# Strassen's seven products in a down-projection: another order, sums made where a block is split, products gathered in SBUF

## The chip, the cores and the metric

One NeuronCore of one Trainium2 chip runs the whole program. The metric is the device time of one execution in microseconds (us), the median of 3 runs. Below, PE is the matrix engine, ACT the scalar engine, DVE the vector engine, SP the queue that issues most of the transfers.

## The reference

Two residual layers on 256 tokens of width 2048, all in float32. Layer 0 mixes tokens with stick-breaking attention, layer 1 with an indexer that selects keys. After each mixer stands the same MLP, and the change touches only the second product of that MLP:

```python
for i in range(DEPTH):                      # DEPTH = 2
    h = rms_norm(x, norm_mix[i])
    x = x + mixer_i(h)                      # stick-breaking, then DSA
    h = rms_norm(x, norm_mlp[i])
    x = x + jnp.square(jax.nn.relu(h @ w_up[i])) @ w_down[i]
```

`w_up` is 2048 x 8192 and `w_down` 8192 x 2048.

## The kernel before

**The work list.** The program is one long list of items. An item is one block of weights, 256 rows by 512 columns, with the matmuls that use it. Activations are held transposed and split in two float32r parts, high and low; a weight block is split the same way. Each product of two 128-row tiles is three matmuls: high x high, high x low, low x high. An ordinary item therefore has 12 matmuls (2 token tiles x 2 row tiles x 3).

**What is done for an item** (the loop at the end of `trunk`, and `load` and `split`, L963 to L996). At item i the program emits, in this order: the split of item i+2, the load of item i+7, the extra loads that hang on the item (`early`), the item's matmuls, the steps that hang on it (`post`), and delayed steps that are due (`later`). A split is a copy on ACT to the high part (L89) and a subtraction on DVE for the low part (L993), with `after` behind it. The two parts lie in a buffer `w` of which there are three: the copy for item i+2 waits until PE has finished item i-1. Loaded blocks lie in `wraw`, of which there are five.

**The order on each engine.** The program is not run in the order in which it is written: a list scheduler puts each engine's instructions in an order before the run, by when it reckons each to be ready, and the earlier one in the program goes first among those that are ready. An instruction wrapped in `keep` cannot stand ahead of the instruction emitted just before it on its engine. Instructions without `keep` (both halves of a split among them) may go earlier or later. On the chip each engine then takes its instructions strictly in that fixed order.

**The MLP.** The 8192 hidden columns are handled in four quarters f. `up(f)` makes 2048 hidden columns in 32 items. A finished group of 512 columns goes through `up_done`: two transposes on DVE (L169), a write to DRAM and a read back, then squared ReLU on DVE (L343), a high part on ACT (L348) and a low part on DVE (L353), each a fixed number of items later. `down(f)` multiplies the quarter by its 2048 rows of `w_down`. The order is up 0, up 1, down 0, up 2, down 1, up 3, down 2, down 3. So the last two groups of the `up` ahead of a `down` still have their ReLU and low parts inside the first pair of that `down`.

**A pair.** `down_pair(f, n)` handles two column groups of 512, G and H, for both token tiles. Of eight row blocks six are ordinary items (G0 to G5, H0 to H5). The other two row blocks (0 and 2) are taken together as a 2 x 2 by 2 x 2 block product in Winograd's form of Strassen's scheme: seven products s1 to s7 of 6 matmuls each in place of eight. The list `TURNS` says how the 19 items follow each other. There are 15 pairs: 8 in the first MLP and 7 in the second, whose last two column groups are done in the ordinary way.

The sums of activations that the scheme needs are made once for each quarter (`sums`). The sums of weight blocks are made in each pair on DVE: three in the `form` of s5, s6 and s7 (L489), one behind the split of s6 (L494). The four blocks are loaded by extra loads on SP (L385) into four tiles of their own, and the seven s-items take nothing from `wraw`.

The products s2, s3 and s4 add to one accumulator each, in PSUM, together with G and H. The products s1, s5, s6 and s7 are shared by several outputs, so each goes to one of two PSUM buffers `aux`, and from there to the residual stream `xs`: s1 is copied to a tile `u` (ACT) and added to one block of `xs`, s5 is added to two, s7 to two at once, and s6 is added to `u`, which is then added to three (L466, L482). That is seven DVE instructions in a pair. When G5 or H5 is done, `down_done` adds its accumulator to `xs` (L305).

## Time and profile before

| | |
|---|---|
| median of 3 runs | 2077.98 us (2077.17 to 2078.2) |
| profiled execution | 2077.52 us, its span 2075.8 us |
| granted PE clock | full |
| transfers | 464.83 MB, mean 224 GB/s |

Times in the profile are us from the start of the span. PE stands for matmuls, PEld for the weight loads that go ahead of them and overlap them. A timeline row holds a start, a duration, the engine, the line, what is written and read, how many instructions are merged in the row, and in brackets how long the engine sat idle before it and what ended that. A matmul's shown duration includes its way through the array, so matmuls overlap in the rows; what counts is the distance from one start to the next.

### The profile page before, as it was taken

How to read it: one execution, taken by the hardware profiler on the slowest of the kernel's cores; microseconds unless marked ns; L12 is line 12 of the kernel's file. 1: busy time of each engine (PE TensorE's matmuls, PEld its weight loads, DVE VectorE, ACT ScalarE, POOL GpSimd, SP SyncE). 2: the span in 40 equal slices, each digit the busy share in tenths (PEclk: the TensorE clock that was granted, in tenths of full speed). 3: DMA queues.
4: the chain of work that ended last, by engine and by line, in shares of the span. 5: the costliest groups of instructions: out<-in, count | busy, mean ns of one | idle time of the engine just before them, and what ended most of it. 6: DMA issues, size and time to landing. Idle time of an engine off the chain costs nothing.

```text
span 2075.8 us, 24805 instructions
## 1 busy us (share of the span) xinstructions
PE 2062.2 (99%) x9164; PEld 1696.1 (82%) x9164; DVE 1467.0 (71%) x1611; ACT 1026.2 (49%) x1233; POOL 26.3 (1%) x71
## 2 busy tenths in 40 slices
PE   9999999999999999999999999999999999999999
PEld 7888888888888888888887788878888888888887
DVE  5556555666696687688885898666669668867885
ACT  6555554544444454445554566554445444444453
POOL 0100000000000000000000000000000000000000
PEclk9999999999999999999999999999999999999999
DMA  9787856988766966876679688498876687677655
GB/s 305 229 235 213 236 172 199 298 250 245 219 208 216 256 206 209 233 211 209 200 216 264 184 250 258 143 265 271 246 242 205 212 238 221 209 216 224 204 176 165
DMA packets 477466, 464.83 MB, mean 224 GB/s; under 512 B 269665, under 2 KB 279969, under 8 KB 477345
## 3 DMA queue, kind: packets, MB, share of 16 engines
q1 hardware_dynamic: 469488, 455.81, 72.3%
q10 hardware_dynamic: 7856, 7.45, 1.2%
q8 instruction: 71, 1.16, 0.2%
q14 instruction: 51, 0.41, 0.1%
HBM read 425.90 MB, written 37.22 MB: 223 GB/s over the span
## 4 chain that ended last, share of the span: by engine, by line
PE 88%; DVE 6%; DMA 2%; issue 2%; ACT 1%; SPq 1%; DVEq 0%; ACTq 0%
PE acc L290 20%; PE acc L291 20%; PE acc L289 20%; PE acc L427 19%; DVE w L993 3%; PE aux L446 2%; DVE xs L466 2%; PE acc L446 1%; ACT w L89 1%; SPq L175 1%; DMA td<-jx 1%; PE acc L259 1%; PE aux L858 1%; DMA wraw<-in_w_up_dram 1%; DVE u L482 0%
## 5 line engine op out<-in xcount | busy, mean ns | idle before, releaser
L993 DVE TENSOR_TENSOR w<-wraw,w 128x1024 fp32r<-128x1024 f32 (+1 forms) x680 | 826.8, 1217 | 506.8 <-ACT w L89 502.0
L89 ACT ACTIVATE w<-wraw 128x1024 fp32r<-128x1024 f32 (+1 forms) x680 | 720.5, 1060 | 860.4 <-PE acc L291 565.0
L290 PE MATMUL acc<-w,xT 128*128 128x512 f32 x1632 | 638.1, 391 | 1.7 <-DVE w L993 1.5
L289 PE MATMUL acc<-w,xT 128*128 128x512 f32 x1632 | 637.1, 391 | 1.9 <-ACT xT L200 1.0
L291 PE MATMUL acc<-w,xT 128*128 128x512 f32 x1632 | 636.3, 390 | 0.0
L427 PE MATMUL acc<-w,hT 128*128 128x512 f32 x2160 | 512.3, 390 | 4.4 <-DVE w L993 3.4
L427 PEld LDWEIGHTS acc<-w,hT 128*128 128x128 f32 x2160 | 404.0, 188 | 96.1 <-DVE w L993 12.4
L289 PEld LDWEIGHTS acc<-w,xT 128*128 128x128 f32 x1632 | 306.4, 188 | 66.8 <-ACT w L89 2.1
L290 PEld LDWEIGHTS acc<-w,xT 128*128 128x128 f32 x1632 | 306.4, 188 | 66.5 <-DVE w L993 2.7
L291 PEld LDWEIGHTS acc<-w,xT 128*128 128x128 f32 x1632 | 306.4, 188 | 64.1 <-issue 0.7
L89 ACT ACTIVATE w<-b 128x1024 fp32r<-128x1024 f32 x105 | 111.5, 1062 | 83.9 <-PE acc L427 61.1
L993 DVE TENSOR_TENSOR w<-b,w 128x1024 fp32r<-128x1024 f32 x105 | 127.8, 1217 | 26.8 <-ACT w L89 26.8
L289 PE MATMUL acc<-w,oT 128*128 128x512 f32 x256 | 100.3, 394 | 0.0
L290 PE MATMUL acc<-w,oT 128*128 128x512 f32 x256 | 99.5, 390 | 0.0
L291 PE MATMUL acc<-w,oT 128*128 128x512 f32 x256 | 99.0, 391 | 0.0
L446 PE MATMUL aux<-w,S 128*128 128x512 f32 x270 | 68.5, 389 | 0.0
L446 PEld LDWEIGHTS aux<-w,S 128*128 128x128 f32 x270 | 50.7, 188 | 10.5
L289 PEld LDWEIGHTS acc<-w,oT 128*128 128x128 f32 x256 | 48.1, 188 | 10.2 <-ACT junk L796 0.4
L290 PEld LDWEIGHTS acc<-w,oT 128*128 128x128 f32 x256 | 48.1, 188 | 9.8
L291 PEld LDWEIGHTS acc<-w,oT 128*128 128x128 f32 x256 | 48.1, 188 | 9.8
L489 DVE TENSOR_TENSOR b<-b,b 128x1024 f32<-128x1024 f32 x45 | 54.8, 1217 | 0.2
L169 DVE STREAM_TRANSPOSE jx<-acc 128x512 f32<-128x512 f32 x68 | 44.6, 694 | 12.0 <-PE acc L291 9.2
(176 smaller groups left out, 1200.0 us busy)
## 6 DMA issues: line engine op xcount, KB each, us to landing
wraw<-in_w_up_dram SPq DMA_DIRECT2D x256, 512.0 KB, 4.4
wraw<-in_w_down_dram SPq DMA_DIRECT2D x196, 512.0 KB, 4.7
wraw<-in_w_in_a_dram SPq DMA_DIRECT2D x94, 512.0 KB, 4.6
wraw<-in_w_in_b_dram SPq DMA_DIRECT2D x64, 512.0 KB, 4.6
td<-jx SPq DMA_DIRECT2D x240, 128.0 KB, 4.3
b<-in_w_down_dram SPq DMA_DIRECT2D x60, 512.0 KB, 4.9
jx<-td SPq DMA_DIRECT2D x45, 512.0 KB, 6.1
wraw<-in_w_out_a_dram SPq DMA_DIRECT2D x32, 512.0 KB, 3.7
```

Of the source, the lines that this page charges most:

```text
L89: pin(act.activation(o, i, AF.Copy, scale=scale))
L169: dve.transpose(y[:, m:m + k, :].rearrange("p k f -> p (k f)"), part)
L175: keep(nc.sync.dma_start(d[:, :, :, a, :].rearrange("b j n i -> j n b i"), y[32 * a:32 * a + 32].rearrange("p n (b i) -> p n b i", b=4)))
L259: pin(pe.matmul(accs[key][t], L[:, j, part, t * P:(t + 1) * P], wx[:, j, :], start=(j == 0 and n == 0), stop=False))
L289: pin(pe.matmul(acc[t], L[:, k, 0, ts], wh[:, j, :], start=(k == 0), stop=False))
L290: pin(pe.matmul(acc[t], L[:, k, 0, ts], wl[:, j, :], start=False, stop=False))
L291: pin(pe.matmul(acc[t], L[:, k, 1, ts], wh[:, j, :], start=False, stop=(k == (end if t else KT) - 1)))
L427: keep(pe.matmul(acc[t], L[:, k, part, ts], wx[:, j, :], start=(i, j, m) == (0, 0, 0), stop=(i, j, m) == (len(qs) - 1, KB - 1, 2)))
L446: keep(pe.matmul(p, left(part, j), wx[:, j, :], start=to is None and (j, m) == (0, 0), stop=to is None and (j, m) == (KB - 1, 2)))
L466: dve.scalar_tensor_tensor(xc, p, sec["rs2"][:, t:t + 1], xc, op0=OP.mult, op1=OP.add)
L489: dve.tensor_sub(x, block(a), block(b))
L993: pin(dve.tensor_sub(wl[:, a], raw[:, a], wh[:, a].bitcast(F32)))
```

## The change

The seven products come in another order, s1 and s3 early and s6 and s5 side by side:

```
before  G0 s1 G1 H0 s5 G2 H1 s7 G3 H2 G4 s6 H3 s3 s2 H4 s4 G5 H5
after   G0 H0 s1 G1 s3 H1 G2 s6 s5 H2 s7 G3 H3 s2 G4 H4 s4 G5 H5
```

Three of the four blocks of weights (of s1, s2, s3) are now loaded into `wraw` like any item's. Only the fourth keeps a tile of its own, Y, loaded by one extra load. The four sums of weight blocks are made behind the split of the item whose block they need, with `keep`: one behind s1, two behind s3, one behind s2, into tiles X, Z and Y. The shared products gather in a tile E of four blocks in SBUF, one block for each token tile and column group: s1 is copied there, s6, s5 and s7 are added with one instruction each, and E is added to `xs` with two instructions, behind G3 and H3. All of these have `keep`. That is five DVE instructions for the products in place of seven.

```diff
-TURNS = "G0 s1 G1 H0 s5 G2 H1 s7 G3 H2 G4 s6 H3 s3 s2 H4 s4 G5 H5".split()
+TURNS = "G0 H0 s1 G1 s3 H1 G2 s6 s5 H2 s7 G3 H3 s2 G4 H4 s4 G5 H5".split()
...
+            def load_y():
+                keep(nc.sync.dma_start(new("Y"), block(1, qa)))
+
+            def t1(b11):
+                keep(dve.tensor_sub(new("X"), sec["Y"], b11))
+
+            def t2_t3(b22):
+                keep(dve.tensor_sub(new("Z"), b22, sec["X"]))
+                keep(dve.tensor_sub(sec["Y"], b22, sec["Y"]))
+
+            def t4(b21):
+                keep(dve.tensor_sub(sec["Z"], b21, sec["Z"]))
 
             def p1(p):
-                sec["u"] = sec["pool"].tile([P, 512], F32, name="u", bufs=1)
-                copy(sec["u"], p)
-                into(0, (0,), p)
+                sec["E"] = sec["pool"].tile([P, 4, 512], F32, name="E", bufs=1)
+                keep(act.activation(sec["E"][:, 0], p, AF.Copy))
+
+            def p6(p):
+                keep(dve.tensor_add(sec["E"][:, 1], p, sec["E"][:, 0]))
 
             def p5(p):
-                for t in range(2):
-                    into(t, (1,), p)
+                keep(dve.tensor_add(sec["E"][:, 2], p, sec["E"][:, 1]))
 
             def p7(p):
-                into(1, (0, 1), p)
...
+                E = sec["E"].rearrange("p (a b) e -> p a b e", a=2)
+                keep(dve.tensor_add(E[:, :, 1], p.unsqueeze(1).to_broadcast([P, 2, 512]),
+                                    sec["E"][:, 1:3]))
+
+            def into(t):
+                xc = xs[:, t, 1024 * n:1024 * n + 1024].rearrange("p (c e) -> p c e", c=2)
+                E = sec["E"].rearrange("p (c t) e -> p c t e", t=2)[:, :, t]
+                keep(dve.scalar_tensor_tensor(xc, E, sec["rs2"][:, t:t + 1], xc,
+                                              op0=OP.mult, op1=OP.add))
...
+            seven["s1"].after, seven["s3"].after, seven["s2"].after = t1, t2_t3, t4
             for name in TURNS:
...
-            for name, col, q, at in (("b11", 0, qa, 8), ("b22", 1, qb, 6), ("b21", 0, qb, 5), ("b12", 1, qa, 3)):
-                items[base - at].early.append(lambda name=name, col=col, q=q: load_block(name, f, n, col, q))
+            items[base - 8].early.append(load_y)
+            for t in range(2):
+                items[base + TURNS.index(("G3", "H3")[t])].post.append(lambda t=t: into(t))
...
             if it.after is not None:
-                it.after()
+                it.after(raw)
```

## The prediction

> **What bounds the kernel now.** I read the page's engine shares first, then the list of waits, then two pairs as windows, then the order of time inside the first pair.

> ```profile
> span 2075.8 us, 24805 instructions
> PE 2062.2 (99%) x9164; PEld 1696.1 (82%) x9164; DVE 1467.0 (71%) x1611; ACT 1026.2 (49%) x1233; POOL 26.3 (1%) x71
> L489 DVE TENSOR_TENSOR b<-b,b 128x1024 f32<-128x1024 f32 x45 | 54.8, 1217 | 0.2
> ...
> PEld acc L427 <- DVE w L993: 12.4, 19, 1.2
> ```
> ```profile
> 559.60:602.30 42.70, 42.53 (x188) 34.83 (x187) 39.18 (x38) 22.61 (x22) 0.00 (x0) 1.00 0.69 216
> 602.30:644.90 42.60, 42.49 (x188) 34.87 (x187) 35.37 (x35) 20.73 (x20) 0.00 (x0) 1.00 0.61 200
> ```

> PE works through the whole span, and the change leaves its matmuls alone: 19 items and 186 matmuls in a pair before and after. So the time can move only by PE's waits. In the pairs these are the 12.4 us in which a weight load waited for the low half of a split; L489 runs 45 times, three in a pair, so there are 15 pairs. The two windows are the two pairs of one quarter (length, then busy time of PE, PEld, DVE, ACT): DVE is busy 39.2 of 42.7 us in the first, 35.4 of 42.6 in the second. DVE has little to spare there, and what stands ahead of a split in its queue decides.

> The next rows give the durations of the whole argument.

> ```profile
> 560.60 1.31 DVE L169 STREAM_TRANSPOSE jx<-acc 128x512 f32<-128x512 f32 x2
> 561.83 1.18 DVE L993 TENSOR_TENSOR w<-wraw,w 128x1024 fp32r<-128x1024 f32 x1
> 562.34 1.52 PE L446 MATMUL aux<-w,hT 128*128 128x512 f32 x6
> 562.54 1.06 ACT L89 ACTIVATE w<-wraw 128x1024 fp32r<-128x1024 f32 x1 [1.65 <-PE acc L427]
> 562.94 1.22 DVE L343 SCALAR_TENSOR_TENSOR jx<-jx 128x1024 f32<-128x1024 f32 x1
> 563.70 5.60 PE L427 MATMUL acc<-w,hT 128*128 128x512 f32 x24
> 563.96 0.60 ACT L89 ACTIVATE u<-aux 128x512 f32<-128x512 f32 x1 [0.35 <-PE aux L446]
> 564.46 1.05 ACT L89 ACTIVATE w<-b 128x1024 fp32r<-128x1024 f32 x1
> 565.41 1.05 ACT L348 ACTIVATE hT<-jx 128x1024 fp32r<-128x1024 f32 x1
> 566.34 0.74 DVE L466 SCALAR_TENSOR_TENSOR xs<-aux,rs,xs 128x512 f32<-128x512 f32 x1
> 566.67 1.06 ACT L89 ACTIVATE w<-wraw 128x1024 fp32r<-128x1024 f32 x1 [0.22 <-ACT hT L348]
> 567.00 1.21 DVE L993 TENSOR_TENSOR w<-b,w 128x1024 fp32r<-128x1024 f32 x1
> 568.13 1.22 DVE L353 TENSOR_TENSOR hT<-jx,hT 128x1024 fp32r<-128x1024 f32 x1
> 569.14 1.52 PE L446 MATMUL aux<-w,S 128*128 128x512 f32 x6
> 569.27 1.22 DVE L993 TENSOR_TENSOR w<-wraw,w 128x1024 fp32r<-128x1024 f32 x1
> ```
> ```profile
> 578.53 1.28 DVE L466 SCALAR_TENSOR_TENSOR xs<-aux,rs,xs 128x1024 f32<-128x1024 f32 x1
> 579.73 1.21 DVE L993 TENSOR_TENSOR w<-wraw,w 128x1024 fp32r<-128x1024 f32 x1
> ...
> 585.76 1.06 ACT L89 ACTIVATE w<-b 128x1024 fp32r<-128x1024 f32 x1 [1.63 <-PE acc L427]
> 586.85 1.23 DVE L993 TENSOR_TENSOR w<-b,w 128x1024 fp32r<-128x1024 f32 x1 [0.33 <-ACT w L89]
> 587.99 0.68 DVE L482 TENSOR_TENSOR u<-aux,u 128x512 f32<-128x512 f32 x1
> 588.60 1.22 DVE L993 TENSOR_TENSOR w<-b,w 128x1024 fp32r<-128x1024 f32 x1
> 589.73 1.94 DVE L466 SCALAR_TENSOR_TENSOR xs<-u,rs,xs 128x512 f32<-128x512 f32 x2
> 591.59 1.22 DVE L993 TENSOR_TENSOR w<-wraw,w 128x1024 fp32r<-128x1024 f32 x1
> ...
> 592.30 0.39 PE L427 MATMUL acc<-w,hT 128*128 128x512 f32 x1
> 592.86 2.79 PE L427 MATMUL acc<-w,hT 128*128 128x512 f32 x11 [0.17 <-DVE w L993]
> 595.49 1.52 PE L446 MATMUL acc<-w,hT 128*128 128x512 f32 x6
> ```

> **A matmul** takes 0.2267 us from start to start: 24 from 563.70 to 569.14. An ordinary item is thus 2.72 us, an s-item 1.36. **The copy** for item i+2 starts 0.20 us after the first matmul of item i (562.34, 562.54): it had waited for the buffer of item i-1. **The subtraction** starts 1.10 us after the copy (585.76, 586.85) if DVE is free. **DVE back to back** moves on every 1.13 us for 1024 columns (567.00, 568.13, 569.27), every 0.61 for the 512-column add (587.99, 588.60), every 1.20 for a 1024-column addition to `xs` (578.53, 579.73), and two transposes take 1.23. **PE goes on** 1.27 us after the subtraction started (591.59, 592.86).

> The last rows are the regular wait of a pair before: H4. Behind two adjacent s-items its second matmul was due at 592.30 + 0.23 = 592.53 and ran at 592.86, 0.33 late, because the two additions of `u` (589.73 to 591.59) stood ahead of its subtraction. The next item began at 595.49, where 592.30 + 12 x 0.2267 = 595.02 was due: 0.47 lost, so a wait costs 0.14 us more than its length. The second window is 0.1 shorter; I take 0.42 for the mean. In 15 pairs: 6.3 us. What else of the 12.4 us lies in the pairs I leave as it is.

> **The change part by part.** *Gone:* the additions of `u` in front of H4. Products cost DVE before 3 x 0.66 + 1.20 (s1, s5, s7) + 0.61 + 0.66 + 1.20 (s6) = 5.65 us in a pair, after 2 x 0.61 + 3 x 1.20 = 4.82: 0.83 less. New forms, such as a 1024-column add of a product into E, are priced by the nearest row (578.53, 1.20). If PE is waiting for nothing, this is worth nothing, so its gain is at most the 0.42 at H4. The adjacent items are now s6 and s5, and the split behind them is H2's: subtraction at 1.30 us after the start of s6, due (2.72 + 0.23 - 1.27) = 1.68 after it, with s6's addition emitted behind it. No wait there.

> *Loads:* 60 blocks as before; 45 of them now pass through the five `wraw` buffers, and load 15 hangs on its own. The shortest five items in a row, s1 G1 s3 H1 G2, last 10.9 us, and a block lands 4.7 to 4.9 us after issue:

> ```profile
> wraw<-in_w_down_dram SPq DMA_DIRECT2D x196, 512.0 KB, 4.7
> b<-in_w_down_dram SPq DMA_DIRECT2D x60, 512.0 KB, 4.9
> ```

> Loads on SP behind a late sum (the block of s3 is free only after the two sums) still have that lead. I take 0 here, and up to 0.3 us a pair for the range; a gain is excluded, since no wait above names these loads.

> *Sums with a fixed place, the part that decides.* Count from G0's first matmul: H0 2.72, s1 5.44, G1 6.80, s3 9.52, H1 10.88. The copy of s3 starts at 5.44 + 0.20 = 5.64, its subtraction at 6.74. Behind it, by `keep`, stand the two new sums at 7.87 and 9.00, and DVE is free at 10.13. H1's copy waits for s1 and stands behind the copy of product s1 (0.50, 563.96 to 564.46): 7.50, so its subtraction could go at 8.60, when the first sum is running and the second already stands ahead. It goes at 10.13; PE gets it at 11.40 and wanted it at 10.88 + 0.23 = 11.11. Wait 0.29, lost 0.43. Before, these sums floated into DVE's idle time; `keep` holds them behind s3's split although their other inputs lie ready long before. This holds for all pairs.

> In the first pair behind an `up` (three quarters in two MLPs: **six pairs**) the held-back ReLU work adds to it. Its low part (L353, 568.13) is now emitted behind the two sums, at 10.13, and H1's subtraction comes behind it. On ACT the high part stood behind the next copy (564.46, 565.41); likewise now copy of s3 5.64, high part 6.59, product copy 7.6, H1's copy 8.1, subtraction ready at 9.2. So it goes at 11.26, PE gets it at 12.53: wait 1.42, lost 1.56. That the low part goes first is what 568.13 shows: G2's copy had started at 566.67, its subtraction could have gone at 567.77, and the low part went ahead of it.

> Further on in these pairs (all starts 1.56 later: s6 17.88, s5 19.24, H2 20.60, s7 23.32, G3 24.68): H2's subtraction 19.18, addition of s6 20.31, s7's subtraction 20.92, addition of s5 22.05, ReLU of the last group 22.66, G3's subtraction 23.79. PE gets it at 25.06 and wanted it at 24.91: wait 0.15, lost 0.29. Then H3's subtraction 24.92, addition of s7 26.05, low part 27.25, s2's subtraction 28.38, the fourth sum 29.51, E to `xs` 30.64, G4's subtraction 31.84. PE gets it at 33.11 and wanted it at 29.92 + 1.85 + 0.23 = 32.00: wait 1.11, lost 1.25. Together 3.10 us. In the other nine pairs the same chain, without ReLU, brings G4's subtraction just in time (29.28 + 1.27 = 30.55 against 30.58).

> **Sum:** 6 x 3.10 + 9 x 0.43 = 22.5 us new, 6.3 us gone: +16.2. The profiled execution took 2077.52 us, 0.46 below the median of 2077.98, so I forecast 2077.5 + 16.2 = **2093.7 us**.

> The rows have DVE moving on every 1.13 us though one instruction lasts 1.22. [...]

> **The rivals.** *Overtaking (2 in 10).* H1's and G4's subtractions are not held by `keep`; the scheduler may see them ready first and put them ahead of the low part and of E's additions. Then the six pairs lose about what the nine do: 15 x 0.43 = 6.45 against 6.3, so 2077.7 us, no change. For: 588.60, where a subtraction went ahead of the additions of `u`, emitted earlier but still waiting for 587.99. Against: 568.13.

> *Gain (2 in 10).* The mechanism is H1's subtraction ahead of the second sum, whose result s7 needs only five items later. It decides at 9.84 us: a subtraction that starts earlier costs PE nothing (11.11 - 1.27). Then the 6.3 us of H4 are gone and nothing takes their place: 2071.2 us. For: DVE's load falls by 0.83 us a pair. Against: the second sum is emitted earlier and ready earlier.

> *Worse (1.5 in 10).* The high part goes ahead of s3's copy, and E's additions slide ahead of G4 in the other pairs too: about 0.5 more in each of six pairs and 0.4 in nine, 2093.7 + 6.6 = 2100.3 us.

> *Nothing happens to the time (inside the overtaking case).* If DVE's queue comes out so that each wait only moves from H4 to H1, the new order and E are real and the time is the same.

> **How the numbers follow.** Forecast 4.5 in 10, worse 1.5, overtaking 2, gain 2. So slower by over 0.2% (about what a measurement of this kernel can tell from no change, 4.2 us) 0.6, within it 0.2, faster 0.2. The forecast's own range is 2087 to 2098. The whole one reaches to the gain's 2071 below, which leaves a deeper gain out, and above to 2102, the worse case with a little of the loads.

> **What would show it.** Right: PE waits at H1's second matmul in every pair, 1.4 us in the six and 0.3 in the nine; a second wait at G4 in the six; two L489-like sums, and in the six the low part, between s3's and H1's subtractions; no wait at H4. Wrong: the low part or the second sum behind H1's subtraction, or pairs as short as 42.2 us. A wait for a `wraw` load in the pairs would mean that I priced the loads wrongly.

## The result and the profile after

The changed kernel takes **2100.9 us** (median of 4 runs, 2098.77 to 2105.26) against 2078.09 us before (4 runs): ratio 1.0112, 95% interval 1.0095 to 1.013. It is slower, by 22.8 us. The profiled execution took 2101.37 us, 23.85 more than that of before. In the page's engine shares PE has the same 9164 matmuls, and DVE got lighter by 12.3 us, 0.82 in each of 15 pairs:

```profile
span 2099.6 us, 24844 instructions
...
PE 2068.1 (99%) x9164; PEld 1697.4 (81%) x9164; DVE 1454.7 (69%) x1581; ACT 1026.3 (49%) x1233; POOL 26.0 (1%) x71
```

So the loss is waiting. The list of waits of after shows for whom: weight loads of the plain products (L419 now) waited 37.2 us for the low half of a split (L994 now), three times the 12.4 of before, in twice the number of waits. The second row is the time that PE itself stood before those matmuls, 22.7 us (3.4 before).

```profile
PEld acc L419 <- DVE w L994: 37.2, 38, 3.3
...
PE acc L419 <- DVE w L994: 22.7, 25, 2.8
```

The same two pairs as windows: the first pair grew from 42.70 to 45.52 us, the second from 42.60 to 42.90 (length, then busy time of PE, PEld, DVE, ACT).

```profile
558.78:604.30 45.52, 43.12 (x187) 34.67 (x186) 38.58 (x36) 22.50 (x22) 0.00 (x0) 1.00 0.65 206
604.30:647.20 42.90, 42.74 (x188) 34.93 (x187) 34.42 (x33) 20.73 (x20) 0.00 (x0) 1.00 0.55 183
```

If each distance from one matmul start to the next is taken, less the bare 0.2267 us, and summed over the plain products, before has 10.4 us too much and after 34.5. The difference, 24.1, is the whole loss. Where it sits is told by the first pair's timelines, DVE first, then PE, then ACT.

```profile
565.75 1.23 DVE L994 TENSOR_TENSOR w<-wraw,w 128x1024 fp32r<-128x1024 f32 x1 [0.94 <-ACT w L89]
566.89 1.22 DVE L469 TENSOR_TENSOR Z<-wraw,X 128x1024 f32<-128x1024 f32 x1
568.03 1.22 DVE L470 TENSOR_TENSOR Y<-wraw,Y 128x1024 f32<-128x1024 f32 x1
569.16 1.22 DVE L353 TENSOR_TENSOR hT<-jx,hT 128x1024 fp32r<-128x1024 f32 x1
570.30 2.36 DVE L994 TENSOR_TENSOR w<-wraw,w 128x1024 fp32r<-128x1024 f32 x2
```
```profile
569.66 0.39 PE L419 MATMUL acc<-w,hT 128*128 128x512 f32 x1
571.58 1.66 PE L419 MATMUL acc<-w,hT 128*128 128x512 f32 x6 [1.52 <-DVE w L994]
```
```profile
563.71 1.06 ACT L348 ACTIVATE hT<-jx 128x1024 fp32r<-128x1024 f32 x1 [0.94 <-DVE jx L343]
564.68 1.04 ACT L89 ACTIVATE w<-wraw 128x1024 fp32r<-128x1024 f32 x1
```

This is H1. s3's subtraction runs at 565.75; behind it stand the two sums and the ReLU's low part; H1's subtraction comes at 570.30. H1's first matmul ran on time at 569.66; the second needs the low half and was due 0.23 later, at 569.89. It ran at 571.58, 1.69 late. On ACT the ReLU's high part (563.71) stood ahead of s3's copy (564.68).

Later in the same pair, at G4, DVE and then PE:

```profile
587.38 1.22 DVE L994 TENSOR_TENSOR w<-wraw,w 128x1024 fp32r<-128x1024 f32 x1
588.51 1.23 DVE L473 TENSOR_TENSOR Z<-wraw,Z 128x1024 f32<-128x1024 f32 x1
589.65 1.29 DVE L493 SCALAR_TENSOR_TENSOR xs<-E,rs,xs 128x1024 f32<-128x1024 f32 x1
590.85 1.23 DVE L994 TENSOR_TENSOR w<-wraw,w 128x1024 fp32r<-128x1024 f32 x1
```
```profile
590.87 0.39 PE L419 MATMUL acc<-w,hT 128*128 128x512 f32 x1
592.13 2.14 PE L419 MATMUL acc<-w,hT 128*128 128x512 f32 x8 [0.87 <-DVE w L994]
```

Between s2's and G4's subtractions lie the fourth sum and the first addition of E to `xs`; G4's second matmul ran 1.03 late. The four first pairs of quarters 0 and 1 look like this one, each with 0.15 more at G3. In the second pairs, and in the first pairs of quarter 3, H1 waits 0.32 and G4 not at all, but for the places named next. No wait is left at H4, and none names a load into `wraw` for the pairs.

Three places are worse than this regular picture. In quarter 2 the first addition of the next sums of `hT` (L390), which has no `keep`, slid in ahead of s3's subtraction. DVE stood 1.13 us at it, until a write to DRAM had read its tile (`td<-jx`), and the whole queue in front of H1 began 1.3 us later than in the regular pair. DVE of after, then the PE row at H1:

```profile
916.42 1.23 DVE L390 TENSOR_TENSOR jx<-hT 128x1024 f32<-128x1024 f32 x1 [1.13 <-DMA td<-jx]
...
917.56 1.22 DVE L994 TENSOR_TENSOR w<-wraw,w 128x1024 fp32r<-128x1024 f32 x1
...
922.10 2.36 DVE L994 TENSOR_TENSOR w<-wraw,w 128x1024 fp32r<-128x1024 f32 x2
...
923.38 5.99 PE L419 MATMUL acc<-w,hT 128*128 128x512 f32 x18 [2.85 <-DVE w L994]
```

H1 waited 3.01 us there and 2.78 in MLP 1. The first of these waits had a sequel. The windows of after (length, busy times of five engines, then the granted clock and the DMA share) show the clock at half for the 3 us that follow, and back after:

```profile
924.80:927.80 3.00, 3.00 (x9) 2.33 (x8) 2.22 (x5) 0.20 (x1) 0.00 (x0) 0.50 0.82 292
927.80:929.80 2.00, 2.00 (x10) 1.67 (x9) 1.11 (x1) 0.86 (x1) 0.00 (x0) 0.99 0.15 58
```

In that stretch the matmuls started every 0.427 us, which cost about 1.5 us. The second place is quarter 2's second pairs, where the last part of the same sums (L399) stood in front of G4: 1.06 each. The third is MLP 0's last pair, where the low parts of the columns turned for the next mixer (L206, four at 1066.87 and four more at 1069.59) stood between splits, in DVE's queue: G3 ran 1.41 late, and G4 behind it 1.50.

```profile
1066.87 1.67 DVE L206 SCALAR_TENSOR_TENSOR xT<-jx,gains,xT 128x256 fp32r<-128x256 f32 x4
1068.45 1.22 DVE L994 TENSOR_TENSOR w<-wraw,w 128x1024 fp32r<-128x1024 f32 x1
1069.59 1.67 DVE L206 SCALAR_TENSOR_TENSOR xT<-jx,gains,xT 128x256 fp32r<-128x256 f32 x4
```

### The profile page after: what moved, and what is told of

The parts are those of the page before. It is cut to its first block, busy times and chain, and to the rows that moved or that the text cites. A ratio compares the mean times of both kernels' runs of the same rounds, so it can differ in the third digit from the quotient of the medians.

```text
span 2099.6 us, 24844 instructions
## 1 busy us (share of the span) xinstructions
PE 2068.1 (99%) x9164; PEld 1697.4 (81%) x9164; DVE 1454.7 (69%) x1581; ACT 1026.3 (49%) x1233; POOL 26.0 (1%) x71
## 3 DMA queue, kind: packets, MB, share of 16 engines
q8 instruction: 72, 1.18, 0.2%
## 4 chain that ended last, share of the span: by engine, by line
PE 86%; DVE 8%; issue 3%; ACT 1%; DMA 1%; SPq 0%; DVEq 0%
PE acc L289 21%; PE acc L290 21%; PE acc L291 21%; PE acc L419 16%; DVE w L994 3%; PE aux L438 1%; PE acc L438 1%; ACT w L89 1%; DVE Y L470 1%; PE acc L259 1%; DVE hT L353 1%; DVE jx L343 1%; DVE xs L493 1%; DVE Z L469 1%; PE aux L859 1%
## 5 line engine op out<-in xcount | busy, mean ns | idle before, releaser
L994 DVE TENSOR_TENSOR w<-wraw,w 128x1024 fp32r<-128x1024 f32 (+1 forms) x725 | 880.8, 1218 | 540.9 <-ACT w L89 534.1
L89 ACT ACTIVATE w<-wraw 128x1024 fp32r<-128x1024 f32 (+1 forms) x725 | 768.3, 1060 | 921.6 <-PE acc L291 587.6
L419 PE MATMUL acc<-w,hT 128*128 128x512 f32 x2160 | 518.1, 392 | 22.7 <-DVE w L994 22.7
L419 PEld LDWEIGHTS acc<-w,hT 128*128 128x128 f32 x2160 | 403.6, 188 | 120.6 <-DVE w L994 37.2
L169 DVE STREAM_TRANSPOSE jx<-acc 128x512 f32<-128x512 f32 x68 | 44.7, 696 | 14.4 <-PE acc L291 12.8
L438 PE MATMUL acc<-w,hT 128*128 128x512 f32 x180 | 45.7, 389 | 0.0
L305 DVE SCALAR_TENSOR_TENSOR xs<-acc,rs,xs 128x512 f32<-128x512 f32 x56 | 39.4, 745 | 8.6 <-PE acc L419 8.6
L438 PEld LDWEIGHTS acc<-w,hT 128*128 128x128 f32 x180 | 33.8, 188 | 7.0
## 6 DMA issues: line engine op xcount, KB each, us to landing
wraw<-in_w_up_dram SPq DMA_DIRECT2D x256, 512.0 KB, 4.2
wraw<-in_w_down_dram SPq DMA_DIRECT2D x241, 512.0 KB, 4.8
wraw<-in_w_in_a_dram SPq DMA_DIRECT2D x94, 512.0 KB, 4.4
wraw<-in_w_in_b_dram SPq DMA_DIRECT2D x64, 512.0 KB, 4.5
jx<-td SPq DMA_DIRECT2D x45, 512.0 KB, 5.9
wraw<-in_w_out_a_dram SPq DMA_DIRECT2D x32, 512.0 KB, 3.7
wraw<-in_w_out_b_dram SPq DMA_DIRECT2D x32, 512.0 KB, 4.7
```

The lines of the kernel that those rows point to most:

```text
L89: pin(act.activation(o, i, AF.Copy, scale=scale))
L169: dve.transpose(y[:, m:m + k, :].rearrange("p k f -> p (k f)"), part)
L305: dve.scalar_tensor_tensor(xc, acc[t], scale[:, t:t + 1], xc, op0=OP.mult, op1=OP.add)
L419: keep(pe.matmul(acc[t], L[:, k, part, ts], wx[:, j, :], start=(i, j, m) == (0, 0, 0), stop=(i, j, m) == (len(qs) - 1, KB - 1, 2)))
L438: keep(pe.matmul(p, left(part, j), wx[:, j, :], start=to is None and (j, m) == (0, 0), stop=to is None and (j, m) == (KB - 1, 2)))
L994: pin(dve.tensor_sub(wl[:, a], raw[:, a], wh[:, a].bitcast(F32)))
```

## The experiments

The theory: the time goes where prerequisite work stands directly in front of the next split in DVE's queue; its place decides, not its amount. Rivals: `keep` as such is what hurts; the gathered E is what hurts; the new order with s6 and s5 side by side is what hurts; the waits only wander, wherever the work stands. All versions start from the changed kernel.

**1. The four sums without `keep`.**

```diff
-                keep(dve.tensor_sub(new("X"), sec["Y"], b11))
+                dve.tensor_sub(new("X"), sec["Y"], b11)
```
(and likewise the other three)

> The changed kernel with the four sums of weight blocks no longer held in place (no keep). Queue theory (sums stand in DVE's queue between s3's and H1's subtraction): the scheduler puts them into idle time, the waits at H1 vanish, those at G4 mostly with them; of about 33 us of waits in the pairs 4 to 6 remain, so about 2075 us. Rival, the new order of items (s6 beside s5, H0 ahead of s1) or the gathering in E is what costs: nothing of that is touched, so 2095 us or more.

Measured: 2122.93 us (2119.27 to 2126.09), ratio 1.0209 (1.0192 to 1.0226). The expectation failed, in size and in sign. The list of waits of this version says why:

```profile
DVE X L466 <- DMA wraw<-in_w_down_dram: 42.5, 15, 6.3
...
DVE Z L473 <- DMA wraw<-in_w_down_dram: 30.3, 15, 3.5
DVE Z L469 <- DMA wraw<-in_w_down_dram: 22.6, 15, 2.4
```

Let go, the sums were put early in DVE's queue, ahead of splits, before their block of weights had landed. DVE takes its queue in order, so it stood 95.4 us at these three (42.5 + 30.3 + 22.6), and the splits behind stood with it, as in its timeline at the fourth sum:

```profile
581.08 1.23 DVE L473 TENSOR_TENSOR Z<-wraw,Z 128x1024 f32<-128x1024 f32 x1 [3.47 <-DMA wraw<-in_w_down_dram]
582.22 1.22 DVE L994 TENSOR_TENSOR w<-wraw,w 128x1024 fp32r<-128x1024 f32 x1
```

So `keep` protects here, and "keep as such hurts" falls.

**2. The third sum moved behind H1's split, with `keep`.**

```diff
             def t2_t3(b22):
                 keep(dve.tensor_sub(new("Z"), b22, sec["X"]))
-                keep(dve.tensor_sub(sec["Y"], b22, sec["Y"]))
+                sec["b22"] = b22
+            def t3(raw):
+                keep(dve.tensor_sub(sec["Y"], sec["b22"], sec["Y"]))
...
+            items[base + TURNS.index("H1")].after = t3
```

> The changed kernel with only the second sum behind s3 (Y) moved behind H1's split, still held in place. Queue theory: H1's subtraction comes one instruction (1.13 us) earlier: its wait falls from 1.69 to 0.55 us in the first pairs behind an up and from 0.32 to nothing in the others, G4's wait stays; about 10 us less, 2091 us. Rivals (order of items, E, loads): no change, 2101 us.

Measured: 2089.35 us (2086.96 to 2092.37), ratio 1.0049 (1.0034 to 1.0064). DVE's timeline has one operation fewer in front of H1's subtraction (the third sum is the row at 570.25; L998 is the split here):

```profile
566.85 1.22 DVE L469 TENSOR_TENSOR Z<-wraw,X 128x1024 f32<-128x1024 f32 x1
567.98 1.22 DVE L353 TENSOR_TENSOR hT<-jx,hT 128x1024 fp32r<-128x1024 f32 x1
569.12 1.22 DVE L998 TENSOR_TENSOR w<-wraw,w 128x1024 fp32r<-128x1024 f32 x1
570.25 1.22 DVE L473 TENSOR_TENSOR Y<-wraw,Y 128x1024 f32<-128x1024 f32 x1
```

H1 waits 0.55 in the four regular first pairs in place of 1.69, one step of DVE (1.13) less, and nothing in the second pairs. G3 and G4 wait as in the changed kernel; in quarter 2's first pairs H1 still waits 1.9. One sum moved by one place gave back about half of the loss.

**3. H1 ahead of s3 in the order.**

```diff
-TURNS = "G0 H0 s1 G1 s3 H1 G2 s6 s5 H2 s7 G3 H3 s2 G4 H4 s4 G5 H5".split()
+TURNS = "G0 H0 s1 G1 H1 s3 G2 s6 s5 H2 s7 G3 H3 s2 G4 H4 s4 G5 H5".split()
```

> The changed kernel with s3 and H1 exchanged in the order, nothing else. Queue theory: the item split right behind the sums is now G2, due 1.36 us later; no wait there in nine pairs and 0.3 us in place of 1.69 in the six; about 11.6 us less, 2089 us. Rival, the adjacent s6 and s5 cost the time: they are still adjacent, 2101 us.

Measured: 2088.15 us (2087.85 to 2089.14), ratio 1.0043 (1.0028 to 1.0058). In DVE's timeline H1's subtraction (568.45) now stands ahead of both sums:

```profile
567.31 1.22 DVE L353 TENSOR_TENSOR hT<-jx,hT 128x1024 fp32r<-128x1024 f32 x1
568.45 1.22 DVE L994 TENSOR_TENSOR w<-wraw,w 128x1024 fp32r<-128x1024 f32 x1
569.58 1.22 DVE L469 TENSOR_TENSOR Z<-wraw,X 128x1024 f32<-128x1024 f32 x1
570.72 1.22 DVE L470 TENSOR_TENSOR Y<-wraw,Y 128x1024 f32<-128x1024 f32 x1
```

No wait of more than 0.11 us is left at H1 or G2 in the pairs of quarters 0 and 1. In quarter 2 H1 still waits 2.1 us behind the slid sums of `hT`, and G4 still waits, 1.03 to 1.08 in the first pairs. The order kept s6 and s5 side by side and gave back over half of the loss, so the rival that blames them explains at most the rest.

**4. E into `xs` two items later (H4 and s4).**

```diff
-                items[base + TURNS.index(("G3", "H3")[t])].post.append(lambda t=t: into(t))
+                items[base + TURNS.index(("H4", "s4")[t])].post.append(lambda t=t: into(t))
```

> The changed kernel with the two additions of E to the residual stream behind H4 and s4 in place of G3 and H3. Queue theory: G4's subtraction is no longer behind an addition, its wait (1.03 us in the six pairs, as much in the second pair of the third quarter) vanishes, H1's waits stay; about 10 us less, 2091 us. Rival, the additions cost DVE time wherever they stand: the wait moves to G5 or the next pair, 2101 us.

Measured: 2097.97 us (2096.79 to 2099.5), ratio 1.009 (1.0075 to 1.0105). G4's waits are gone in all regular pairs and H1's unchanged at 1.69 and 0.32, as expected, but the total missed by 7 us: the long wait at H1 in quarter 2 was 3.05 us in both MLPs, each with matmuls at a lower granted clock behind it (0.50 from 923.4 to 925.4, a mean of 0.65 from 1930.5 to 1933.5), and in MLP 0's last pair a new wait of 3.30 appeared (1067.68), again with slow matmuls behind it (the seven from 1068.94 took 3.28 us, where 6 x 0.2267 + 0.39 makes 1.75). There ACT had stood 3.59 us at a high part of the turned columns (L200) until its read from DRAM had landed, with three copies behind it. A wait at G5 or in the next pair, as the rival had it, did not come in the regular pairs.

**5. The old products in the new order.** E is taken out: u, and each product added to `xs` on its own, as before.

```diff
             def p6(p):
-                keep(dve.tensor_add(sec["E"][:, 1], p, sec["E"][:, 0]))
+                u = sec["u"]
+                dve.tensor_add(u, p, u)
+                into(0, (1,), u)
+                into(1, (0, 1), u)
```
(p1, p5 and p7 likewise as before, and E's two additions at G3 and H3 taken out)

> The new order and the kept sums as in the kernel after, but the products go the old way: u in SBUF from s1, each product added to xs on its own, the two additions of u behind s6. Theory (the place of instructions in DVE's queue decides, and the gathered E is the part of the change that saves): DVE carries 0.83 us a pair more, and all of s6's three operations and s5's two now stand in the queue between H2's and G3's subtractions, so new waits come at s7, H2 or G3 on top of those at H1: 2110 to 2135 us. Rival (E is what costs: its copy, its additions over 1024 columns and its late move into xs): below 2095 us, and no wait at G4.

Measured: 2129.44 us (2128.82 to 2134.3), ratio 1.0247 (1.0232 to 1.0263). A row of its list of waits, where L996 is the split, and DVE's timeline at H1:

```profile
PEld acc L419 <- DVE w L996: 61.7, 51, 4.0
```
```profile
567.77 1.22 DVE L470 TENSOR_TENSOR Y<-wraw,Y 128x1024 f32<-128x1024 f32 x1
568.91 0.74 DVE L480 SCALAR_TENSOR_TENSOR xs<-aux,rs,xs 128x512 f32<-128x512 f32 x1
569.57 1.22 DVE L353 TENSOR_TENSOR hT<-jx,hT 128x1024 fp32r<-128x1024 f32 x1
570.70 2.35 DVE L996 TENSOR_TENSOR w<-wraw,w 128x1024 fp32r<-128x1024 f32 x2
```

s1's addition to `xs` (568.91) stands in front of H1 as well, and H1 waits 2.34; G3 now waits 0.28, H3 0.7 and G4 1.5, and H1 of the second pairs 0.98. In the new order the changed kernel's products are 28.5 us faster than the old ones, and "E hurts" falls. The old products also stand without `keep`, as before; how much of the 28.5 us is E and how much is their held place, no run tells.

**6. The sums of `hT` held at their place.**

```diff
-            dve.tensor_add(a, hi.bitcast(F32), lo.bitcast(F32))
+            keep(dve.tensor_add(a, hi.bitcast(F32), lo.bitcast(F32)))
```

> Only the first addition of the sums of hT is held at its place, so that in quarter 2 it cannot slide ahead of s3's subtraction. Theory: the waits of 3.0 and 2.8 us at H1 in quarter 2's first pairs shrink to the 1.69 of the other first pairs, and the stretch of matmuls at half clock behind the 3.0 us goes with it: 2.4 + 1.5 = 3.9 us less, 2096 to 2098 us; the waits elsewhere stay. Rival (the long wait has another cause, or the held sums make a wait of the same size where they now stand, at the end of quarter 2): 2100 to 2103 us.

Measured: 2093.64 us (2092.41 to 2094.7), ratio 1.0067 (1.0053 to 1.0081). At quarter 2's H1 the wait is now the regular one, and the clock stays full (mean of the run 1.000, against 0.998):

```profile
920.32 0.39 PE L419 MATMUL acc<-w,hT 128*128 128x512 f32 x1
922.23 0.97 PE L419 MATMUL acc<-w,hT 128*128 128x512 f32 x3 [1.52 <-DVE w L994]
```

It gave 7.3 us, more than expected: besides the two long waits and the half clock, the 1.06 at G4 of quarter 2's second pairs went too, since L399 no longer stood there. Summed over the plain products as above, 28.3 us are too much in place of 34.5, so 6.3 us of the gain lie in the pairs.

**7. Moves 3, 4 and 6 together**, with E's additions left at G3 and H3 in MLP 0's last pair; **8.** the same with them late there too.

```diff
-                items[base + TURNS.index(("G3", "H3")[t])].post.append(lambda t=t: into(t))
+                items[base + TURNS.index((("G3", "H3") if f == 3 and n else ("H4", "s4"))[t])].post.append(lambda t=t: into(t))
```

> Three moves together, keep and E left in: H1 ahead of s3 in the order (no sums in front of H1's subtraction), the sums of hT held at their place, and E's additions to xs at H4 and s4 instead of G3 and H3 (but not in MLP 0's last pair, where moving them cost a wait). Theory: from the 2088.2 of the swap alone, 6 x (1.06 + 0.11) = 7.0 us at G4 and some 5 at quarter 2 go: 2075 to 2078 us, so no slower than the kernel before, and perhaps faster by 1 to 3 us. Rival (the new products and sums cost DVE places wherever they stand, so the waits only wander): above 2083 us.

> The same, with E's additions at H4 and s4 in MLP 0's last pair too. Theory: with H1 ahead of s3 the last pair has no sums in front of H1, so the 1.5 us at its G4 goes and the 3.3 us that the late additions brought there without the swap may come back in part: within 2.5 us of the other version, 2073 to 2080 us. Rival: the 3.3 us wait and half clock are back, 2079 us or more.

Measured: version 7 2077.79 us (2075.98 to 2079.49), ratio 0.9993 (0.9984 to 1.0002); version 8 2079.89 us (2077.29 to 2083.19), ratio 1.0004 (0.9995 to 1.0013). The whole loss is back, with the sums still held by `keep` and E still there, so "the waits only wander" falls, and so does the blame on s6 and s5, which are still side by side. The waits that are left lie mostly in MLP 0's last pair. ACT, then PE, of version 7:

```profile
1056.58 1.70 ACT L200 ACTIVATE xT<-jx,gains 128x256 fp32r<-128x256 f32 x4 [4.39 <-DMA jx<-td]
1058.19 2.94 ACT L89 ACTIVATE w<-wraw 128x1024 fp32r<-128x1024 f32 x3
```
```profile
1059.28 0.50 PE L419 MATMUL acc<-w,hT 128*128 128x512 f32 x1 [3.94 <-ACT w L89]
```

As in experiment 4, ACT stood 4.39 us at a read from DRAM, and three copies went only afterwards. In version 8 the wait that its rival named is back (3.22 us; the mean granted clock of that run was 0.997), but version 7, without the late additions there, has it too (4.10), so they are not its cause.

**9 and 10. Versions 7 and 8 with two items more between that read and its use.**

```diff
-                later(4, then, z)
+                later(lag, then, z)
...
-            add_residual(g, next_col if f == 3 else None, acc, sec["rs2"])
+            add_residual(g, next_col if f == 3 else None, acc, sec["rs2"], 0, 6 if g < 2 else 4)
```
(`lag` is 4 elsewhere)

> The three moves of the version with H1 ahead of s3 (2077.8 us), and in MLP 0's last pair the high parts of the turned columns 0 to 1 stand six items behind their read from DRAM instead of four. Theory: the 4.1 us that PE lost there at 1059 us came from ACT, which stood 4.39 us at such a high part until its read had landed, with two copies behind it; with two more items of lead the read has landed, so the 4.1 us, the 1.0 behind them and six matmuls at half clock (1.2 us) go, 6.3 us: 2070 to 2073 us, faster than the kernel before by 0.25 to 0.4%. Rival (the wait only moves on, because the low parts now stand ahead of H3's or G4's subtraction): 2075 to 2078 us, no difference from the kernel before.

> The same with E's additions at H4 and s4 in MLP 0's last pair too. Theory: the 1.0 to 1.5 us at G4 of the last pair that the additions at G3 and H3 may still cost there are gone: 2070 to 2073 us, within 1.5 us of the other. Rival (late additions hold xs columns or DVE for the turned columns): 2075 us or more.

Measured: version 9 2075.58 us (2073.23 to 2076.99), ratio 0.9983 (0.9974 to 0.9992); version 10 **2074.88 us** (2072.91 to 2079.41), ratio 0.9984 (0.9976 to 0.9993). Both beat the kernel before, by 0.16 to 0.17% with the intervals clear of 1, but both missed the expected 2070 to 2073 us. Version 9 lies where its rival put it. ACT's wait for that read shrank from 4.39 us to 0.40 in version 9 and 1.49 in version 10. As the rival had it, the wait moved on: the low parts of the turned columns now stand in front of G4's subtraction, in version 9 with an addition of E, and G4 waits 3.54 us in version 9 and 2.19 in version 10. The regular pairs of version 10 are as short as the prediction's case "gain" would have them; PE is busy in all of a bare pair of 186 x 0.2267 = 42.17 us, and the waits for splits fell to a quarter of the changed kernel's:

```profile
558.78:600.95 42.17, 42.17 (x185) 34.23 (x184) 37.37 (x36) 22.51 (x22) 0.00 (x0) 1.00 0.69 216
600.95:643.20 42.25, 42.25 (x188) 35.00 (x187) 34.48 (x33) 20.73 (x20) 0.00 (x0) 1.00 0.60 187
```
```profile
PEld acc L419 <- DVE w L994: 9.2, 16, 2.5
```

## Why the prediction was right, and where it was short

- **Slower, and why: right.** DVE's queue between s3's and H1's subtractions came out as written: sum, sum, low part. Experiments 2 and 3 show that this queue is the cause: taking one sum out of it shortened the wait by one step of DVE, taking both out ended it.
- **The time: too low, and partly by luck on the right side.** 2100.9 us lies above the forecast's own range (2087 to 2098) and almost on the price of the case "worse" (2100.3). That case's mechanism does not explain it: of its two halves only the first came, and a regular first pair lost 0.1 us more than forecast, where the case had 0.5. The rest came from places that no case had priced.
- **DVE's saving of 0.83 us a pair: right in size** (0.82). H4's waits went, as predicted. That the saving by itself is worth no more than H4's wait was not tried. In the new order the old products cost 28.5 us more (experiment 5), which the prediction did not ask.
- **The wait at H1 in the six pairs: mis-sized, 1.42 against 1.69.** The step that failed is "on ACT the high part stood behind the next copy ... likewise now". It stood ahead of it (563.71 and 564.68), so s3's subtraction came 0.23 later. That was the first half of the rival "worse"; its second half, E's additions sliding ahead of G4 in the other pairs, did not come.
- **G3, G4 and the nine pairs: right, outside quarter 2 and the last pair.** 0.15 at G3 as predicted, 1.03 at G4 against 1.11; 3.20 us lost in a regular first pair (1.69 + 0.15 + 1.03 and 0.11 for each restart) against 3.10. In the nine pairs 0.32 at H1 against 0.29.
- **The step that made the sum too small** (+16.2 against +23.85) is the factors in 6 x 3.10 + 9 x 0.43: all first pairs were priced alike, and all others alike. In quarter 2 the sums of `hT` for the next quarter also stand in DVE's queue, and the prediction has them nowhere. Of the missing 7.65 us, quarter 2's first pairs took 4.4 (3.01 and 2.78 instead of 1.42, and 1.5 at half clock), quarter 2's second pairs 2.3 (2 x (1.06 + 0.11) at G4), and the four regular pairs 0.4. About 0.5 us is not placed. Experiment 6 confirms the first two: one `keep` in front of the sums of `hT` gave 7.3 us.
- **"What else of the 12.4 us lies in the pairs I leave as it is": right in size by luck.** The irregular waits did not stay. Four of before went (0.92, 0.54, 0.60 and 0.89 us, in quarter 2's first pairs and MLP 0's last pair), and three came in MLP 0's last pair (0.15, 1.41, 1.50). With the restarts both come to 3.4 us.
- **The loads: right.** No split in the pairs waited for `wraw`. That holds only while the sums are held: in experiment 1, standing earlier in the queue, three of the four waited 95.4 us for their blocks.
- **The rival "gain" did not come.** The second sum stayed ahead of H1's subtraction. Its 2071.2 us is neared only by versions with four further moves (2074.88, with 2.2 us and more still lost in MLP 0's last pair).
- **DVE's step.** Rows 566.89, 568.03, 569.16 and 570.30 are again 1.13 to 1.14 apart with durations of 1.22, as the prediction took them.

## What to carry to other kernels

When an engine works through its queue in order, ask of every instruction whose time is not pressing which pressing one it stands directly in front of. Here moving two such sums behind the next item's split was worth 13 us, while the change as a whole made DVE 12.3 us lighter and the kernel 22.8 us slower. Pinning an instruction has two sides: it keeps a sum from blocking the queue for a transfer that has not landed (DVE stood 95.4 us at such sums in experiment 1), but the place must lie behind the next item's split, and its neighbours that are not pinned may slide into the new gaps (the sums of `hT` in quarter 2, where DVE stood 1.13 us). Add irregular places (a stage's last pair, the pair in which the next stage's sums are made) to a prediction one by one; pricing them like the others was the largest error here.

## What was not expected of the hardware

The granted clock fell to 0.50 behind some waits of PE. Behind the 3.01 us in the changed kernel it did, with a matmul every 0.427 us in place of 0.2267, so that this wait cost about 1.5 us more than its length. It did behind 2.87 us just after MLP 0 too (0.50 from 1115.59 to 1119.00); behind the 2.78 in MLP 1 it did not (1.00). In experiment 3 it did behind one of the two waits of 2.1 us (0.50 from 923.00 to 925.30) and not behind the other (1.00 from 1923.20 to 1926.50); in version 9 it did behind 3.54 (0.50 from 1066.40 to 1069.40), in version 10 not behind 2.19 (1.00 from 1063.40 to 1066.40). So the length of a wait alone does not decide among these.

```profile
921.04:924.45 3.41, 1.07 (x5) 0.90 (x6) 3.41 (x5) 0.41 (x1) 0.00 (x0) 1.00 0.47 163
924.45:927.86 3.41, 3.41 (x10) 2.65 (x9) 2.57 (x6) 0.26 (x1) 0.00 (x0) 0.50 0.80 274
1927.97:1931.38 3.41, 2.59 (x12) 1.82 (x10) 3.41 (x4) 2.02 (x2) 0.00 (x0) 1.00 0.72 280
1931.38:1934.79 3.41, 1.61 (x7) 1.36 (x8) 3.41 (x4) 0.10 (x1) 0.00 (x0) 1.00 0.58 189
```

Of the wait of 3.01 us, 2.34 lay in one interval, and the next interval ran at a clock of 0.50. The 2.78 us were cut by a border at 1931.38 into 0.98 and 1.80 (from start to start), and the clock stayed at 1.00. In experiment 3 the wait that was followed by half clock lay whole in one interval, the other was cut into 0.90 and 1.21. PE's idle time in each interval (start to start, less 0.2267 us), counted in the traces of before and after: the four intervals with the most of it, 2.98, 2.54 and 2.47 us in after (from 1112.18, 2095.22 and 921.03) and 2.04 in before (from 2070.94), are each followed by a clock of 0.50; of the others whose sequel the clock's record holds, with 1.93 or less, none is. So in these two traces it is the idle time within one interval that matches; no run was made to test it.
